# Index queries of a sparse-attention layer: from rows of tokens to columns of tokens, and only for tokens 64 to 255

## The chip, the core and the metric

The kernel runs on one core of one Trainium2 chip. The metric is the device time of one execution in microseconds (us); a comparison of two kernels is a ratio of such times, taken on the same chip. The engines of the core have short names throughout: PE is the matrix engine (PEld its weight loads), V or DVE the vector engine, A or ACT the scalar engine, G or POOL the GpSimd engine, SP the engine whose queue issues the loads from memory.

## What is computed

The reference is two layers of a decoder trunk on 256 tokens of width 1024. A layer is a half-step feed-forward block, a mixer, and another half-step feed-forward block. The mixer projects the normed tokens once and feeds three groups of attention heads. The change concerns the group A, whose 4 query heads attend only to keys that an indexer picks:

```python
iq = apply_rope(iq.reshape(B, S, IDX_HEADS, IDX_DIM), cos, sin)     # 8 indexer heads of 64
ik = apply_rope(ik.reshape(B, S, 1, IDX_DIM), cos, sin)[:, :, 0]    # one shared indexer key
...
topk = min(DSA_TOPK_MAX, S // 4)                                    # 64
idx_logits = jnp.einsum('bqhe,bse->bqhs', qib, ki_f)
score = jnp.einsum('bqh,bqhs->bqs', wib * DSA_IDX_SCALE, jax.nn.relu(idx_logits))
score = jnp.where(causal[None], score, -jnp.inf)
_, sel = lax.top_k(score, topk)
valid = sel <= qpos[None, :, None]
```

A query at position p has p + 1 admissible keys. For the first 64 positions that is at most 64, so the 64 picked keys contain all of them and what is attended to is the causal mask itself, whatever the scores are.

## The kernel before

Tokens stand on partitions, in two tiles of 128 (t = 0, 1). Each weight is split into a high and a low part (`wh` by an ACT cast, L125; `wl` by a DVE subtraction, L129), and so are the normed activations (`norm.h`, `norm.l`, two halves of one tile `norm.x`); a product is three matmuls, high by high, high by low and low by high (`mm3`, L340, over `mm`, L338). The splitting is kept ahead of use by a small planner (`Weights`, L64): `take()` hands out the next unit, `pump()` (L101) puts one more cast on ACT and one subtraction, a unit behind, on DVE, unless seven units are already ahead. A unit has 1024 columns in most places, 672 in the chunk `ib` and 768 in the chunk `a`.

The mixer (L688) goes through eight chunks of the input projection in the order of `CHUNKS` (L51): iq, ib, b, a, ck, cq, cv, cg. A chunk has four units of weights and each unit is one step: 12 matmuls, in which 128 tokens are the stationary operand and up to 512 features the moving one, so that a result has tokens on partitions. Beside the chunks runs other work of the mixer: `at_step(n, fn)` (L692) puts a function on a list, and `run_side()` (L695) after each unit issues those whose step has come. This is program order; each engine then works through its own instructions strictly in that order, and an instruction that waits holds up all that is behind it on its engine.

What happens to the index queries (`post_iq`, L760) after the four steps of the chunk iq: ACT copies the two banks to four tiles of 128x256 with the norm's factor (`evac`, L737); `rope` (L704) turns them by position along the free dimension, with two products on G into a tile `swapped` (L710, L711; two such tiles in turn, shared with all other uses of `rope`) and a product and a sum on DVE (L712, L713); at step 9 PE transposes them in 16 pieces of 64 rows (L179), and ACT copies the result to `iqT`, features on partitions and tokens along the free dimension.

After the chunk ib, at step 8, `post_ib` (L773) issues the same for the single index key: `rope` on `ix` (L786, through L710 to L713), then a copy that doubles it into `ikd` (L787). At step 10 PE transposes `ikd` (`turn_ik`, L818, the transposes in L821), at step 11 it computes the products of `iqT` and `ikT` for the second tile of queries (`index(1)`, L826), and DVE sums them into `score` (L842). At step 18 (`B_TURN`) the same is done for the first tile, and in steps 15 to 30 `topk` takes the largest eight scores eight times over. `amask` (L858) makes the mask of the A heads from what was taken.

At the start of the mixer the second half of the normed activations is still to be made: `norm.half(1)` (L376), with eight PE transposes (L373), runs within the first step, and `norm.sums()` after the second.

Of the kernel before, what the change touches and what calls it, by code (L numbers as in the profile page):

```python
# [10 lines left out]
F32 = mybir.dt.float32  # L11
# [3 lines left out]
ALU = mybir.AluOpType  # L15
# [3 lines left out]
P = 128  # L19
S = 256  # L20
# [4 lines left out]
DEPTH = 2  # L25
HD = 64
TOPK = 64
EPS = 1e-6
NEG = -1e30
IDX_SCALE = (8 ** -0.5) * (64 ** -0.5)  # L30
# [20 lines left out]
CHUNKS = [  # L51
    ("iq", [(384, 512, 0)]),
    ("ib", [(896, 328, 0), (3272, 8, 328)]),
    ("b", [(1224, 512, 0)]),
    ("a", [(0, 384, 0)]),
    ("ck", [(2248, 512, 0)]),
    ("cq", [(1736, 512, 0)]),
    ("cv", [(2760, 512, 0)]),
    ("cg", [(3280, 512, 0)]),
# [94 lines left out]
def kernel(ctx: ExitStack, tc: tile.TileContext, x, ffn1_norm, ffn1_w_gate, ffn1_w_up, ffn1_w_down,  # L154
# [3 lines left out]
    cp = ctx.enter_context(tc.tile_pool(name="cp", bufs=1))  # L158
# [3 lines left out]
    hp = ctx.enter_context(tc.tile_pool(name="hp", bufs=HID_BUFS))  # L162
    tp = ctx.enter_context(tc.tile_pool(name="tp", bufs=9))
    sm = ctx.enter_context(tc.tile_pool(name="sm", bufs=4))
    at = ctx.enter_context(tc.tile_pool(name="at", bufs=1))
# [5 lines left out]
    V, A, G, T = nc.vector, nc.scalar, nc.gpsimd, nc.tensor  # L171

    def bank(tag):
        return psum.tile([P, 512], F32, name="ps_" + tag, tag=tag)

    def turn(ps, i, src):
        for e, b in enumerate(ps):
            r = slice(64 * e, 64 * e + 64)
            T.transpose(b[:, 64 * i:64 * i + 64], src[r], ident[r, r])  # L179

    def turned(ps, dst, copies):
        for e, copy in enumerate(copies):
            d = dst[..., 64 * e:64 * e + 64]
            n = 64
            for k in d.shape[1:-1]:
                n *= k
            src = ps[e][:, :n]
            if len(d.shape) == 3:
                src = src.rearrange("p (b j) -> p b j", j=64)
            else:  # L190
                src = src.rearrange("p (a b j) -> p a b j", a=d.shape[1], j=64)
            copy(d, src)

    def by_block(ap):
        return ap.rearrange("p h (t c) -> p (h t) c", c=P)
# [3 lines left out]


    trunk = xp.tile([P, 2, D], F32, name="trunk")
    cst = cp.tile([P, 384], F32, name="cst")
    ident = cp.tile([P, P], F32, name="ident")
    rows, more_rows = tmp(P)[:16], tmp(P)[:32]
    gT = cp.tile([P, 48], F32, name="gT")
# [32 lines left out]
    W = Weights(tc, raw_pool, split_pool)  # L238
# [85 lines left out]

    future = cst[:, 0:P]
    cs = cst[:, P:3 * P].rearrange("p (t c) -> p t c", t=2)
    causal = cp.tile([P, 3 * P], F32, name="causal")
    cqa = [at.tile([P, 8, HD], F32, name=f"cqa{t}", tag=f"cqa{t}") for t in range(2)]
    cka = [at.tile([P, 8, HD], F32, name=f"cka{t}", tag=f"cka{t}") for t in range(2)]
# [15 lines left out]
    def rsqrt(dst, src, per, n, tag):  # L345

        y = sm.tile([P, 32], F32, name="y_" + tag, tag="y_" + tag, bufs=1)[:, :n]
        V.tensor_scalar(dst, src, per, EPS, op0=ALU.mult, op1=ALU.add)  # L348
        G.tensor_tensor(y, dst, minus_half[:, :n], op=ALU.pow)  # L349
# [338 lines left out]
    def mixer(l, norm, nxt):  # L688
        side, count = [], itertools.count()
        step = [0]  # L690

        def at_step(n, fn):  # L692
            side.append((n, next(count), fn))
# [7 lines left out]
        def heads(ap, n):  # L701
            return ap.rearrange("p (h d) -> p h d", h=n)

        def rope(x, ta, tb, E=G):  # L704

            n = x.shape[1]
            bc = lambda a: a[:, None, :].to_broadcast([P, n, a.shape[1]])
            b = tp.tile([P, S], F32, name="swapped", tag="swapped", bufs=2)
            b = heads(b[:, :n * HD], n)
            G.tensor_tensor(b[:, :, 0:32], x[:, :, 32:64], bc(tb[:, 0:32]), op=ALU.mult)  # L710
            G.tensor_tensor(b[:, :, 32:64], x[:, :, 0:32], bc(tb[:, 32:64]), op=ALU.mult)  # L711
            E.tensor_tensor(x, x, bc(ta), op=ALU.mult)  # L712
            E.tensor_tensor(x, x, b, op=ALU.add)  # L713
# [22 lines left out]
        def evac(dst, ps, t, scale=None):  # L736
            A.activation(dst, ps, AF.Copy, scale=norm.r[:, t:t + 1])  # L737
# [3 lines left out]
        def pairs_T(dst, *xs):  # L741

            ps = [bank("acc") for _ in range(2)]
            i = itertools.count()
            for x in xs:
                for j in range(0, x[0].shape[1], P):
                    for t in range(2):
                        turn(ps, next(i), x[t][:, j:j + P])
            turned(ps, by_block(dst), (A.copy, A.copy))
# [7 lines left out]
        st = {}  # L757


        def post_iq(ps):  # L760
            rot = [[hp.tile([P, S], F32, name="iqr", tag="hl") for _ in range(2)] for t in range(2)]
            for t in range(2):
                for jj in range(2):
                    evac(rot[t][jj], ps[t][:, jj * S:(jj + 1) * S], t)
                    rope(heads(rot[t][jj], 4), cs[:, t, 0:64], cs[:, t, 64:128], V)

            def turn_iq():
                st["iqT"] = at.tile([P, 4, S], F32, name="iqT", tag="kT")
                pairs_T(st["iqT"], *[[rot[t][jj] for t in range(2)] for jj in range(2)])

            at_step(9, turn_iq)

        def post_ib(ps):  # L773
            ss = sm.tile([P, 2, 4], F32, name="ssbq", tag="ss")
# [3 lines left out]
            small = [at.tile([P, 80], F32, name=f"ix{t}", tag=f"ix{t}") for t in range(2)]  # L778
            rot = [hp.tile([P, S], F32, name="bqr", tag="hl") for _ in range(2)]
# [4 lines left out]
            for t in range(2):  # L784
                x = small[t][:, None, 0:64]
                rope(x, cs[:, t, 0:64], cs[:, t, 64:128], V)  # L786
                V.tensor_copy(ikd[t], x.to_broadcast([P, 2, HD]))  # L787
                V.tensor_tensor(fg[:, t], small[t][:, 72:80], fb[:, l], op=ALU.add)
                V.tensor_scalar(st["iw"][:, t], small[t][:, 64:72], IDX_SCALE, None, op0=ALU.mult)
            sq = []  # L790
            for t in range(2):
                evac(rot[t], ps[t][:, 72:328], t)
# [65 lines left out]
            def amask():  # L858
                am = at.tile([P, 3 * P], F32, name="amask", tag="amask")
                V.tensor_scalar(am[:, P:2 * P], st["score"][1][:, 0:P], -2e38, None, op0=ALU.is_gt)  # L860
                for t in range(2):
                    V.scalar_tensor_tensor(am[:, 2 * t * P:(2 * t + 1) * P], st["score"][t][:, t * P:(t + 1) * P],
                                           -2e38, future, op0=ALU.is_gt, op1=ALU.max)
                V.tensor_scalar(am, am, NEG, None, op0=ALU.mult)
                st["amask"] = am

            for r in range(TOPK // 8):
                at_step(TOP_STEP + 2 * r, lambda: topk(1))
# [288 lines left out]
        def both_scores(_):  # L1157
            for fn in (scores, st["B"][0]):
                for p in range(2):
# [4 lines left out]
                    b=lambda p: st["B"][1](p), B=lambda p: st["B"][2](p), T=lambda _: tanh(), w=causal_part)  # L1164
# [6 lines left out]
        at_step(A_STEP + 1, lambda: do("q j"))  # L1171

        oT = {}
        posts = dict(iq=post_iq, ib=post_ib, a=post_a, b=post_b, ck=post_ck, cq=post_cq, cv=post_cv, cg=post_cg)
        for name, cols in CHUNKS:
            n = sum(c[1] for c in cols)
            ps = [bank("gu") for _ in range(2)]
            for u in range(4):
                w = W.take()
                for kk in range(2):  # L1180
                    k = 2 * u + kk
                    for t in range(2):
                        ts = slice(t * P, (t + 1) * P)
                        mm3(ps[t][:, :n], (norm.h[:, k, ts], norm.l[:, k, ts]), [v[:, kk] for v in w],
                            k == 0, k == KT - 1)
                    if name == "iq" and k == 0:
                        norm.half(1)
                if name == "iq" and u == 1:
                    norm.sums()
                step[0] += 1  # L1190
                run_side()
                if step[0] < A_STEP:
                    W.pump(2 if name == "iq" else 1)
            posts[name](ps)
        while side:
            step[0] += 1
# [63 lines left out]
        def norm_out(_):  # L1260
# [5 lines left out]
            for t in range(2):  # L1266
# [3 lines left out]
                    p=lambda _: W.pump(), Z=residuals, N=norm_T, M=norm_out)  # L1270
# [21 lines left out]
    norm = Norm(0, 0)  # L1292
    turn_gains()
    for l in range(DEPTH):
        norm = ffn(norm, lambda: Norm(1, l), lambda: before_mixer(l), l == 0)
        norm = mixer(l, norm, lambda: Norm(2, l))
        norm = ffn(norm, (lambda: Norm(0, l + 1)) if l + 1 < DEPTH else None)
# [7 lines left out]
def _constants(np):  # L1305

    inv = (1.0 / np.power(10000.0, np.arange(0, HD, 2, dtype=np.float64) / HD)).astype(np.float32)
    ang = np.arange(S, dtype=np.float32)[:, None] * inv[None, :]
    c, s = np.cos(ang), np.sin(ang)
    rot = np.concatenate([c, c, -s, s], axis=1).astype(np.float32).reshape(2, P, P)  # L1310
    i = np.arange(P)
    return np.ascontiguousarray(np.concatenate([i[None, :] > i[:, None], rot[0], rot[1]], axis=1), dtype=np.float32)


# [17 lines left out]
```

## Time and profile before

| | |
|---|---|
| median of three runs | 1008.81 us (1008.67 to 1008.81) |
| span of the profiled execution | 1007.0 us |
| first index-query matmul to the transpose of `ikd`, layer 1 | 192.04 to 217.51 us of the span |
| the same, layer 2 | 690.35 to 715.82 us |

The profile belongs to one execution. It gives no time of its own beside the span; the span runs from its first to its last instruction, and the runs' times are 1.7 to 1.8 us longer than that. The chain of waits is followed back from the last instruction, each time to what released it. A row of the timeline has the start and the length in us, the engine, the line, the operation, what it writes and reads, the shape and how many instructions of the same kind it merges; the last entry, in brackets, is the idle time before it and what ended it. Lengths of matmuls are modelled ends, so what a matmul costs in a stream is read from the distance of starts.

### The profile page before, as it was taken

What the parts mean: (1) busy time and instruction counts of PE and PEld (TensorE: products, weight loads), DVE (VectorE), ACT (ScalarE), POOL (GpSimd) and SP (SyncE); (2) the same over time, 40 slices, a digit from 0 to 9 for tenths busy, and PEclk for the clock granted to TensorE, in tenths of its full rate; (3) what the DMA queues carried; (4) which work ended last, traced back from release to release, by engine and by line L of the source; (5) the groups of instructions that cost most, each with busy time, mean ns of one, the idle gap of its engine ahead of it and who ended that gap; (6) DMA issues with size and microseconds to landing.
All of it is one profiled execution on the core that took longest, in us unless ns stands there. A gap on an engine that the chain in (4) does not pass through costs nothing.

```text
span 1007.0 us, 15203 instructions
## 1 busy us (share of the span) xinstructions
PE 1002.5 (100%) x5692; PEld 857.6 (85%) x5692; DVE 795.0 (79%) x1474; ACT 590.6 (59%) x1090; POOL 164.5 (16%) x192
## 2 busy tenths in 40 slices
PE   9999999999999999999999999999999999999998
PEld 8888888888878888888888888888887788888887
DVE  5978778779998777777878777787899877777775
ACT  6655555567776555555465555556678765555552
POOL 2003000068812000000000020001778120000000
PEclk9999999999999999999999999999999999999999
DMA  9764746464625455655645655665556255374731
GB/s 289 264 225 157 233 147 237 140 241 168 221 94 168 156 178 174 203 188 199 199 168 180 203 182 195 197 197 175 182 204 230 72 179 170 131 242 141 237 127 42
DMA packets 133497, 184.60 MB, mean 183 GB/s; under 512 B 7152, under 2 KB 106928, under 8 KB 133424
## 3 DMA queue, kind: packets, MB, share of 16 engines
q1 hardware_dynamic: 133392, 183.62, 55.1%
q8 instruction: 45, 0.74, 0.3%
q14 instruction: 28, 0.23, 0.1%
q10 hardware_dynamic: 32, 0.01, 0.0%
HBM read 182.55 MB, written 1.06 MB: 182 GB/s over the span
## 4 chain that ended last, share of the span: by engine, by line
PE 98%; DVE 1%; ACT 0%; issue 0%; POOL 0%; POOLq 0%
PE ps_gu L338 67%; PE ps_acc L338 29%; PE ps_acc L373 1%; PE ps_acc L179 1%; DVE wl L129 0%; PE ps_gu L179 0%; DVE p L1078 0%; PE ps_acc L535 0%; DVE ol L1138 0%; PE ps_acc L940 0%; PE ps_acc L400 0%; DVE cT L1240 0%; DVE cT L1236 0%; ACT oh L1130 0%; PE ps_acc L821 0%; PE ps_acc L875 0%
## 5 line engine op out<-in xcount | busy, mean ns | idle before, releaser
L129 DVE TENSOR_TENSOR wl<-raw,wh 128x1024 fp32r<-128x1024 f32 (+2 forms) x342 | 416.9, 1229 | 25.2 <-ACT wh L125 25.1
L125 ACT CAST wh<-raw 128x1024 fp32r<-128x1024 f32 (+2 forms) x341 | 341.7, 1036 | 19.1 <-PE ps_gu L338 9.3
L338 PE MATMUL ps_gu<-xhl,wh 128*128 128x512 f32 x1408 | 330.8, 390 | 0.0
L338 PEld LDWEIGHTS ps_gu<-xhl,wh 128*128 128x128 f32 x1408 | 263.1, 188 | 54.0 <-ACT wh L125 0.4
L338 PEld LDWEIGHTS ps_gu<-xhl,wl 128*128 128x128 f32 x1408 | 176.0, 191 | 4.0
L338 PE MATMUL ps_gu<-xhl,wl 128*128 128x256 f32 x1408 | 178.7, 283 | 0.0
L482 DVE TENSOR_TENSOR tmp<-ps_gu,tmp 128x256 f32<-128x256 f32 x176 | 72.9, 423 | 108.9 <-ACT tmp L481 108.6
L338 PE MATMUL ps_gu<-wh,xhl 128*128 128x512 f32 (+2 forms) x512 | 155.1, 378 | 0.0
L338 PE MATMUL ps_acc<-wh,hh 128*128 128x512 f32 (+1 forms) x352 | 137.2, 390 | 0.0
L338 PE MATMUL ps_acc<-wl,hh 128*128 128x512 f32 (+1 forms) x352 | 137.1, 389 | 0.0
L338 PE MATMUL ps_acc<-wh,hl 128*128 128x512 f32 (+1 forms) x352 | 136.5, 388 | 0.0
L481 ACT COPY tmp<-ps_gu 128x256 f32<-128x256 f32 x176 | 63.4, 371 | 91.5 <-PE ps_gu L338 91.2
L338 PEld LDWEIGHTS ps_gu<-wh,xhl 128*128 128x128 f32 x512 | 94.6, 188 | 16.8 <-issue 1.7
L496 ACT CAST hh<-tmp 128x256 fp32r<-128x256 f32 x80 | 32.6, 407 | 120.3 <-DVE tmp L493 120.3
L338 PE MATMUL ps_gu<-wl,xhl 128*128 128x512 f32 (+2 forms) x256 | 95.7, 374 | 0.0
L488 ACT ACTIVATE tmp<-tmp 128x256 f32<-128x256 f32 x88 | 36.9, 419 | 83.3 <-DVE tmp L486 83.1
L349 POOL TENSOR_TENSOR y_n<-msq,minus_half 128x2 f32<-128x2 f32 x6 | 7.0, 1174 | 443.8 <-DVE msq L348 443.8
L338 PEld LDWEIGHTS ps_acc<-wh,hl 128*128 128x128 f32 x352 | 66.1, 188 | 13.9
L338 PEld LDWEIGHTS ps_acc<-wh,hh 128*128 128x128 f32 x352 | 66.2, 188 | 12.6
L338 PEld LDWEIGHTS ps_acc<-wl,hh 128*128 128x128 f32 x352 | 66.3, 188 | 12.4 <-DVE wl L129 0.2
L338 PEld LDWEIGHTS ps_gu<-wl,xhl 128*128 128x128 f32 x256 | 48.2, 188 | 6.9
L506 DVE TENSOR_TENSOR tmp<-tmp,rb 128x256 f32<-128x256 f32 x88 | 37.5, 426 | 3.0
(232 smaller groups left out, 899.2 us busy)
## 6 DMA issues: line engine op xcount, KB each, us to landing
raw<-in_ffn_w_down_dram SPq DMA_DIRECT2D x44, 1024.0 KB, 4.9
raw<-in_ffn_w_gate_dram SPq DMA_DIRECT2D x42, 1024.0 KB, 6.9
raw<-in_ffn_w_up_dram SPq DMA_DIRECT2D x42, 1024.0 KB, 7.7
raw<-in_w_in_dram SPq DMA_DIRECT2D x24, 1024.0 KB, 5.0
raw<-in_w_out_dram SPq DMA_DIRECT2D x8, 1024.0 KB, 5.0
raw<-in_w_in_dram SPq DMA_DIRECT2D x4, 768.0 KB, 4.9
raw<-in_w_in_dram SPq DMA_DIRECT2D x4, 656.0 KB, 4.0
raw<-in_ffn_w_gate_dram SPq DMA_DIRECT2D x3, 512.0 KB, 7.7
```

Source lines behind the costliest of these rows:

```text
L125: self.nc.scalar.copy(hv, src)
L129: (engine or self.nc.vector).tensor_tensor(lv, self.srcs[self.n_low], hv.bitcast(F32), op=ALU.subtract)
L179: T.transpose(b[:, 64 * i:64 * i + 64], src[r], ident[r, r])
L338: T.matmul(o, l, r, start=start, stop=stop, skip_group_check=True)
L349: G.tensor_tensor(y, dst, minus_half[:, :n], op=ALU.pow)
L373: T.transpose(ps[:, i, t * P:(t + 1) * P], trunk[:, t, (2 * mp + i) * P:(2 * mp + i + 1) * P], ident)
L481: A.copy(o, ps[:, 1])
L482: V.tensor_tensor(o, ps[:, 0], o, op=ALU.add)
L488: A.activation(th, t_, AF.Tanh, scale=0.5)
L496: (V.tensor_copy if late else A.copy)(hh, t_)
L506: V.tensor_tensor(t_, t_, norm.rb, op=ALU.mult)
```

## The change

The chunk iq leaves the loop over chunks. A new function does it in four steps ahead of the loop, with the weights as the stationary operand (128 features at a time, f = 0 to 3) and the tokens 64 to 255 as the moving one: one matmul of 2 x 192 columns takes high and low activations against the high weights, one of 192 columns takes the high activations against the low weights. The result has features on partitions and needs no transposition. The rotation then acts along partitions: G multiplies 32 partitions at a time, with the other half's partitions as input, in 16 instructions of 32x192 for the four f; DVE does four products and four sums of 128x192. The columns of `iqT` of the first 64 tokens are set to zero. The norm's factor is left out of the queries and put on the indexer's head weights instead. In the mask the first 64 rows are copied from the causal one. The constants get two more tables of 192 columns.

```diff
-        def post_iq(ps):
-            rot = [[hp.tile([P, S], F32, name="iqr", tag="hl") for _ in range(2)] for t in range(2)]
-            for t in range(2):
-                for jj in range(2):
-                    evac(rot[t][jj], ps[t][:, jj * S:(jj + 1) * S], t)
-                    rope(heads(rot[t][jj], 4), cs[:, t, 0:64], cs[:, t, 64:128], V)
-
-            def turn_iq():
-                st["iqT"] = at.tile([P, 4, S], F32, name="iqT", tag="kT")
-                pairs_T(st["iqT"], *[[rot[t][jj] for t in range(2)] for jj in range(2)])
-
-            at_step(9, turn_iq)
+        def index_queries():
+
+            ps = [bank("gu")[:, :2 * LATE].rearrange("p (a s) -> p a s", a=2) for _ in range(4)]
+            qs = [hp.tile([P, S], F32, name="iqr", tag="hl")[:, :LATE] for _ in range(4)]
+            iqT = st["iqT"] = at.tile([P, 4, S], F32, name="iqT", tag="kT")
+            G.memset(iqT[:, :, :TOPK], 0.0)
+            for u in range(4):
+                w = W.take()
+                for f in range(4):
+                    fs = slice(f * P, (f + 1) * P)
+                    for kk in range(2):
+                        mm(ps[f], w[0][:, kk, fs], norm.x[:, 2 * u + kk, :, TOPK:], u + kk == 0, False)
+                    for kk in range(2):
+                        mm(ps[f][:, 0], w[1][:, kk, fs], norm.h[:, 2 * u + kk, TOPK:], False, u + kk == 4)
+                    if u == 0 and f == 1:
+                        norm.half(1)
+                    if u == 3:
+                        o = tmp(LATE)
+                        A.copy(o, ps[f][:, 1])
+                        V.tensor_tensor(qs[f], ps[f][:, 0], o, op=ALU.add)
+                if u == 1:
+                    norm.sums()
+                step[0] += 1
+                run_side()
+                W.pump(2)
+            swapped = [tp.tile([P, S], F32, name="swapped", tag="swapped", bufs=2)[:, :LATE] for _ in range(2)]
+
+            def turned_part(f):
+                b = swapped[f % 2]
+                for i in range(4):
+                    to, of = slice(32 * i, 32 * i + 32), slice(32 * (i ^ 1), 32 * (i ^ 1) + 32)
+                    G.tensor_tensor(b[to], qs[f][of], csT[of, 1], op=ALU.mult)
+
+            def straight_part(f):
+                V.tensor_tensor(iqT[:, f, TOPK:], qs[f], csT[:, 0], op=ALU.mult)
+
+            def added(f):
+                V.tensor_tensor(iqT[:, f, TOPK:], iqT[:, f, TOPK:], swapped[f % 2], op=ALU.add)
+
+            for f in range(2):
+                turned_part(f)
+            for f in range(4):
+                straight_part(f)
+            for f in range(2):
+                at_step(5, lambda f=f: added(f))
+                at_step(5, lambda f=f: turned_part(2 + f))
+                at_step(7, lambda f=f: added(2 + f))
...
-                V.tensor_scalar(st["iw"][:, t], small[t][:, 64:72], IDX_SCALE, None, op0=ALU.mult)
+                V.tensor_scalar(st["iw"][:, t], small[t][:, 64:72], IDX_SCALE, norm.r[:, t:t + 1], op0=ALU.mult,
+                                op1=ALU.mult)
...
+                V.tensor_copy(am[:TOPK, 0:P], future[:TOPK])
                 for t in range(2):
-                    V.scalar_tensor_tensor(am[:, 2 * t * P:(2 * t + 1) * P], st["score"][t][:, t * P:(t + 1) * P],
-                                           -2e38, future, op0=ALU.is_gt, op1=ALU.max)
+                    r = slice(TOPK if t == 0 else 0, P)
+                    V.scalar_tensor_tensor(am[r, 2 * t * P:(2 * t + 1) * P], st["score"][t][r, t * P:(t + 1) * P],
+                                           -2e38, future[r], op0=ALU.is_gt, op1=ALU.max)
...
-        for name, cols in CHUNKS:
+        index_queries()
+        for name, cols in CHUNKS[1:]:
...
-                    W.pump(2 if name == "iq" else 1)
+                    W.pump()
```

`TOPK` is 64 and `LATE` is 192. The products of `iqT` and `ikT`, the sums of the scores and the rounds of `topk` keep their number and sizes.

More of the change, by code (lines that the diff above doesn't have):

```diff
@@ L27 @@
 TOPK = 64
+LATE = S - TOPK
 EPS = 1e-6
@@ L201 @@
     trunk = xp.tile([P, 2, D], F32, name="trunk")
-    cst = cp.tile([P, 384], F32, name="cst")
+    cst = cp.tile([P, 3 * P + 2 * LATE], F32, name="cst")
     ident = cp.tile([P, P], F32, name="ident")
@@ L326 @@
     cs = cst[:, P:3 * P].rearrange("p (t c) -> p t c", t=2)
+    csT = cst[:, 3 * P:].rearrange("p (i s) -> p i s", i=2)
     causal = cp.tile([P, 3 * P], F32, name="causal")
@@ L1173, in mixer @@
         oT = {}
-        posts = dict(iq=post_iq, ib=post_ib, a=post_a, b=post_b, ck=post_ck, cq=post_cq, cv=post_cv, cg=post_cg)
-        for name, cols in CHUNKS:
+        posts = dict(ib=post_ib, a=post_a, b=post_b, ck=post_ck, cq=post_cq, cv=post_cv, cg=post_cg)
+        index_queries()
+        for name, cols in CHUNKS[1:]:
             n = sum(c[1] for c in cols)
@@ L1185, in mixer @@
                             k == 0, k == KT - 1)
[L1186 to L1189, printed above, removed]
                 step[0] += 1
@@ L1311, in _constants @@
     i = np.arange(P)
-    return np.ascontiguousarray(np.concatenate([i[None, :] > i[:, None], rot[0], rot[1]], axis=1), dtype=np.float32)
+    late = np.concatenate([np.concatenate([c, c, c, c], axis=1).T, np.concatenate([s, -s, s, -s], axis=1).T], axis=0)
+    late = late.reshape(2, P, S)[:, :, TOPK:].transpose(1, 0, 2).reshape(P, 2 * LATE)
+    return np.ascontiguousarray(np.concatenate([i[None, :] > i[:, None], rot[0], rot[1], late], axis=1),
+                                dtype=np.float32)
 def kernel(**inputs):
```

## The prediction

> **What bounds the kernel now.** I read the page first: its busy times and the chain of waits.
>
> ```profile
> span 1007.0 us, 15203 instructions
> PE 1002.5 (100%) x5692; PEld 857.6 (85%) x5692; DVE 795.0 (79%) x1474; ACT 590.6 (59%) x1090; POOL 164.5 (16%) x192
> PE 98%; DVE 1%; ACT 0%; issue 0%; POOL 0%; POOLq 0%
> ```
>
> The chain is PE from end to end, so matmul time removed is gained at once, unless PE afterwards arrives somewhere before its input does. POOL's 16% is an average; the next view, sums by stretch, shows the stretch in question, from the first index-query matmul (192.04) to the end of the chunk ib.
>
> ```profile
> core 0: us, PE busy (x) PEld busy (x) DVE busy (x) ACT busy (x) POOL busy (x), PEclk, DMA share, GB/s
> 192.04:203.81 11.77, 11.77 (x57) 9.84 (x56) 10.20 (x15) 9.51 (x18) 1.21 (x1) 1.00 0.41 130
> 203.81:211.20 7.39, 7.39 (x50) 7.38 (x49) 5.85 (x11) 4.82 (x10) 4.02 (x8) 1.00 0.80 291
> ```
>
> The clock is full (1.00), the index queries take PE 11.77 us, ib 7.39. DVE is busy for 10.20 of the first 11.77. What PE meets next is read from the timeline, of PE and of DVE, in both layers:
>
> ```profile
> 192.04 0.39 PE L338 MATMUL ps_gu<-wh,xhl 128*128 128x512 f32 x1
> 217.51 0.38 PE L821 MATMUL ps_acc<-ident,ikd 128*128 128x128 f32 x2
> 690.35 0.39 PE L338 MATMUL ps_gu<-wh,xhl 128*128 128x512 f32 x1
> 715.82 0.38 PE L821 MATMUL ps_acc<-ident,ikd 128*128 128x128 f32 x2
> 209.48 4.21 DVE L129 TENSOR_TENSOR wl<-raw,wh 128x1024 fp32r<-128x1024 f32 x4
> 213.61 0.27 DVE L712 TENSOR_TENSOR ix<-ix,cst 128x64 f32<-128x64 f32 x1
> 215.39 0.78 DVE L787 COPY ikd<-ix 128x128 f32<-128x128 f32 x1
> ```
>
> This is what decides. The transpose of `ikd` starts at 217.51, and DVE has `ikd` ready at 215.39 + 0.78 = 216.17: PE arrives only 1.34 us after its input. DVE took the index key up at 213.61, behind four splits of weights. Counted from the first index-query matmul (I call that time T), PE is at T+25.47 and `ikd` at T+24.13, and in layer 2 PE is at T+25.47 again. What the change saves on PE beyond 1.34 us is worth nothing if `ikd` stays where it is, and costs if `ikd` moves back.
>
> **PE's part.** Distances of starts price a matmul in a stream.
>
> ```profile
> 153.67 3.83 PE ps_gu L338 x32
> 177.71 10.88 PE ps_acc L338 x48
> 228.19 0.33 PE L338 MATMUL ps_gu<-wl,xhl 128*128 128x384 f32 x1
> 232.87 0.33 PE L338 MATMUL ps_gu<-wl,xhl 128*128 128x384 f32 x1
> 274.08 0.60 PE L940 MATMUL ps_acc<-ident,aqr 128*128 128x128 f32 x4
> 274.51 0.38 PE L940 MATMUL ps_acc<-ident,akd 128*128 128x128 f32 x2
> ```
>
> The first two are pieces of the chain: 32 matmuls of 256 columns (the feed-forward block's narrow ones) at 0.120 us each, 48 of 512 at 0.227. Between the next two lie nine groups of three of 384 columns: 4.68 / 27 = 0.173. A line through these gives 0.093 at 192 columns. But four 128-column transposes start 0.109 apart (0.43 / 4), longer than their columns alone would take by that line: a load of new weights with each instruction seems to set a floor. I take 0.109. Before, 48 matmuls x 0.227 = 10.88. After, 32 x 0.173 + 32 x 0.109 = 9.03. With the 0.86 us of the eight transposes of `norm.half(1)`, which both kernels have in this stage, the queries end at T+9.89 instead of T+11.77. `half(1)` stands after 8 of the new matmuls (1.13 us) where it stood after 6 of the old (1.36), so what follows it on ACT and DVE is 0.23 earlier too, and its results are still due only at the third unit, over 3 us later: free.
>
> ```profile
> 213.69 0.39 PE L338 MATMUL ps_gu<-wh,xhl 128*128 128x512 f32 x1
> 214.01 0.71 PE L179 MATMUL ps_acc<-ident,iqr 64*128 64x64 f32 x16
> 214.65 0.50 PE L338 MATMUL ps_gu<-wh,xhl 128*128 128x512 f32 x1
> 214.99 0.39 PE L338 MATMUL ps_gu<-wl,xhl 128*128 128x512 f32 x1
> ```
>
> The transposes of the queries go: from 213.69 to 214.99 is 1.30, of which two matmuls are 0.45, so 0.85 us.
>
> Something comes back at once. The new function takes all four banks of its kind, so ib must wait until DVE has summed the first.
>
> ```profile
> 198.66 4.66 DVE L129 TENSOR_TENSOR wl<-raw,wh 128x672 fp32r<-128x672 f32 x5
> 192.85 1.22 DVE L129 TENSOR_TENSOR wl<-raw,wh 128x1024 fp32r<-128x1024 f32 x1
> 206.06 0.41 DVE L712 TENSOR_TENSOR iqr<-iqr,cst 128x256 f32<-128x256 f32 x1
> ```
>
> Four of the five splits of the first row are queued ahead of these sums (the fourth step's is behind). They end at 203.32 less some 1.2 for the last, T+10.06, with the shift T+9.83. By the other two rows DVE needs (1.22 - 0.41) / 768 = 1.055 ns a column and 0.14 us besides, so 0.34 for a sum of 192. ib starts at T+10.17 instead of T+9.89. Then 7.39 for ib and 24 x 0.227 = 5.44 for two steps of b: PE stands before `ikd` at **T+23.0**, against T+25.47. That is the whole gain, 2.47 us a layer.
>
> **When `ikd` is ready.** DVE must do, in order: the sums, a split, four straight products, two `added`, two splits, two `added`, two splits, and then the index key. Each `added` waits for four instructions of G, and G for DVE (the third and fourth `turned_part` write buffers that `added` has read). So all 16 instructions of G lie ahead of `ikd`, where there were 8 shorter ones.
>
> ```profile
> 203.95 0.46 POOL L710 TENSOR_TENSOR swapped<-iqr,cst 128x128 f32<-128x128 f32 x1 [3.85 <-ACT iqr L737]
> 204.37 0.46 POOL L711 TENSOR_TENSOR swapped<-iqr,cst 128x128 f32<-128x128 f32 x1
> 220.05 0.73 POOL L713 TENSOR_TENSOR bqr<-bqr,swapped 128x256 f32<-128x256 f32 x1
> 217.31 1.25 POOL L711 TENSOR_TENSOR swapped<-bqr,tab 128x128 f32<-128x128 f32 x1
> 217.29 2.09 DVE L129 TENSOR_TENSOR wl<-raw,wh 128x768 fp32r<-128x768 f32 x2
> 211.91 0.97 POOL L711 TENSOR_TENSOR swapped<-ix,cst 128x32 f32<-128x32 f32 x1
> ```
>
> Alone, G needs 0.46 us for 128 columns and 0.73 for 256: 2.1 ns a column and 0.19 besides. While DVE runs splits (two inputs from SBUF), the 128 columns take 1.25, and 32 columns 0.97. So the two engines take turns, and their columns add up. A check on before: from G's first (203.95) to DVE's taking up `ix` (213.61), 9.66 us, DVE did 8 x 256 + 2 x 1024 + 2 x 768 = 5632 columns (5.94 us) and G 8 x 128 + 3 x 32 = 1120 (2.35), together 8.29; the other 1.37 are fixed parts and waits. From there to `ikd` were 2.56.
>
> After, from G's first at about T+10.3: DVE 1024 + 4 x 192 + 4 x 192 + 2 x 1024 + 2 x 768 = 6144 columns, 6.48 us; G 16 x 192 + 96 = 3168 columns, 6.65; together 13.1. That assumes that 32 partitions cost G what 128 do; no row shows fewer than 128. With nothing for fixed parts `ix` is taken up at T+23.4 and `ikd` is ready at T+26.0; stretched as before (9.66 / 8.29) it is T+25.6 and T+28.2. Laid out instruction by instruction, one engine after the other on its columns and 0.07 (DVE) or 0.15 (G) ahead of each, the kernel before gives T+24.2 (measured 24.13) and the changed one **T+27.5**. I take that, being nearest to a measured case. PE, there at T+23.0, waits 4.5 us and goes on 2.1 us later than before.
>
> Nothing behind that is due sooner than PE: the profile has DVE idle before the scores, so its delay is taken up there.
>
> ```profile
> 222.37 0.48 DVE L842 SCALAR_TENSOR_TENSOR score<-tmp,iw,causal 128x256 f32<-128x256 f32 x1 [2.99 <-ACT tmp L838]
> ```
>
> The rest I cost at nothing: ACT's four 128x192 copies for four of 128x256, and two of 128x512 dropped (ACT is at 59%); the memset on an idle G; the head weights' second factor; the small copy in `amask`; the larger constants, one load in the feed-forward block before. With cover gone the copy in `amask` would be 0.3 us a layer.
>
> **Sum.** 2 x (+2.1) = +4.2 us on the profiled span of 1007.0, and as both lie 1.8 apart, on the median 1008.8: **1013.0 us**. Its own range goes from no fixed parts (2 x 0.5: 1009.8) to 1016 (stretched as before, 2 x 2.7, and some more for G).
>
> **Rivals.**
>
> First, *faster*: the four quarter instructions of a `turned_part` touch different partitions and overlap, or cost less than whole ones. If the 16 take under 0.3 us each instead of 0.56 (192 x 2.1 ns + 0.15), `ikd` is ready by T+23 and all 2.47 us land in each layer: 1008.8 - 4.9 = 1003.9. Against it: in the rows of G independent instructions start 0.42 apart where one lasts 0.46, hardly any overlap; but those use all partitions. The Trainium skill, "GPSIMD Engine Reference", section Instruction dispatch, says that a core of G serves 16 fixed partitions and starts the next instruction as soon as its own share is done. By that the quarters would overlap, and the result would be this rival's; no row here shows it. I give 0.25.
>
> Second, *much slower*: all matmuls of the trace on split operands (written as fp32r, as the rows of L129 show) have 256 columns or more; the only shorter matmuls that are not transposes are plain fp32, at another price.
>
> ```profile
> 220.57 2.00 PE L338 MATMUL ps_acc<-ikT,iqT 64*128 64x256 f32 x16
> 222.50 0.50 PE L338 MATMUL ps_gu<-wh,xhl 128*128 128x512 f32 x1
> ```
>
> Eight products of 256 columns, two at a time, take 1.93 us: 0.48 a pair. If 192 columns in fp32r went at that pace, 0.36 instead of 0.109, the queries would end at T+17.9 and PE reach `ikd` at T+30.7; laid out the same way it is ready at T+33.8, +8.4 us a layer, 1025.6; with G's overlap +5.3, 1019.4. For it is only that no row speaks against it; the 256-column row, the nearest, lies on the line. I give 0.20.
>
> Third, *no difference*: G somewhat cheaper, 1.5 ns a column, so that the wait (2 us) eats the gain: 1008. I give 0.10.
>
> That leaves 0.45 for the forecast.
>
> **How the numbers follow.** A measurement here tells 0.2%, 2 us, from no change. Faster: the first rival, 0.25. Same: the third and the forecast's lower edge, 0.13. Slower: the rest, 0.62. The range runs from the first rival's 1003.9, a little lower for a narrow matmul on the line, to the second's milder case: 1003.3 to 1019.5; what is left out is the second rival's worse case, 0.15, and some of the tails.
>
> **What would show it.** In the changed profile: starts of the 192-column matmuls about 0.11 apart; ib's first matmul near T+10.2; G's 32x192 at 0.6 us, longer beside splits, the last ending near T+22.4; and PE idle for some 4.5 us before L821 in each layer, with DVE and POOL in the chain there. If PE does not wait there and stands at T+23, the price of G was wrong; if the queries end at T+18, the price of the narrow matmul.

## The result and the profile after

The changed kernel takes 1020.83 us (median of four runs, 1019.68 to 1021.4), the kernel before 1008.74: 1.0119 times as long, 95% interval 1.0104 to 1.0133. The forecast was 1013.0 with a range up to 1019.5. The sign was right; the size was some three times what was forecast.

The changed kernel's lines are numbered anew: `mm` is L340, the splits L130, G's quarter products L793, DVE's straight products L796, `added` L799, the copy into `ikd` L824, its transposes L859, the scores L880.

The profile page of the changed kernel, its span, busy times and chain:

```profile
span 1019.7 us, 15219 instructions
PE 1003.7 (98%) x5692; PEld 860.0 (84%) x5692; DVE 801.0 (79%) x1484; ACT 586.7 (58%) x1086; POOL 180.8 (18%) x210
PE 91%; DVE 3%; POOL 3%; issue 1%; DMA 1%; ACT 1%; SPq 0%; POOLq 0%; DVEq 0%
```

PE's share of the chain has gone from 98% to 91%; DVE's has gone from 1% to 3% and POOL's from 0% to 3%. The timeline of PE shows where: the query matmuls, the start of ib, the transposes of `ikd` in layer 1, and the first score products.

```profile
197.41 0.54 PE L340 MATMUL ps_gu<-xhl,wh 128*128 128x384 f32 x2
...
197.98 0.54 PE L340 MATMUL ps_gu<-xhl,wh 128*128 128x384 f32 x2
...
202.22 0.42 PE L340 MATMUL ps_gu<-wh,xhl 128*128 128x336 f32 x1
...
214.93 0.39 PE L340 MATMUL ps_gu<-wh,xhl 128*128 128x512 f32 x1
219.12 0.47 PE L859 MATMUL ps_acc<-ident,ikd 128*128 128x128 f32 x1 [3.80 <-DVE ikd L824]
220.86 0.47 PE L859 MATMUL ps_acc<-ident,ikd 128*128 128x128 f32 x1 [1.27 <-DVE ikd L824]
...
221.56 0.63 PE L340 MATMUL ps_gu<-wl,xhl 128*128 128x512 f32 x1
221.99 1.05 PE L340 MATMUL ps_gu<-wh,xhl 128*128 128x512 f32 x2
222.84 0.63 PE L340 MATMUL ps_gu<-wl,xhl 128*128 128x512 f32 x1
...
226.17 1.13 PE L340 MATMUL ps_acc<-ikT,iqT 64*128 64x256 f32 x8
```

One f of the queries costs 197.98 - 197.41 = 0.57 (forecast 2 x 0.173 + 2 x 0.109 = 0.564). T is 191.99 here, so ib starts at T+10.23 (forecast T+10.17), and after its last matmul before `ikd`, at 214.93 + 0.23 = 215.16, PE stands at T+23.2 (forecast T+23.0). PE's part is as the prediction had it. Then PE waits 3.80 and 1.27 us for `ikd`. Layer 2 shows the same pair of waits.

```profile
723.99 0.33 PE L859 MATMUL ps_acc<-ident,ikd 128*128 128x128 f32 x1 [3.80 <-DVE ikd L824]
725.74 0.47 PE L859 MATMUL ps_acc<-ident,ikd 128*128 128x128 f32 x1 [1.42 <-DVE ikd L824]
```

What the prediction had no term for stands behind the waits: three matmuls of 512 columns from 221.56 to 222.84 take 1.28 us, 0.427 each, where the same instruction took 0.227. The sums by stretch name the reason, first of the changed kernel, then of the kernel before:

```profile
215.00:220.00 5.00, 0.79 (x3) 0.18 (x1) 3.76 (x10) 0.00 (x0) 4.47 (x8) 0.90 0.42 134
220.00:225.00 5.00, 4.14 (x11) 3.27 (x12) 4.62 (x9) 1.32 (x2) 4.76 (x6) 0.50 0.54 197
225.00:230.00 5.00, 5.00 (x28) 3.70 (x27) 1.86 (x4) 2.67 (x5) 2.13 (x3) 0.91 0.63 210
```

```profile
220.00:225.00 5.00, 5.00 (x30) 3.70 (x29) 2.35 (x5) 3.26 (x6) 2.81 (x3) 1.00 0.62 210
```

The column ahead of the last two is the granted clock. It is 0.50 from 220 to 225; narrow stretches of this trace read either 1.00 or 0.50, so a missing share counts twice, and PE spends about 2 x 0.10 x 5 + 5 + 2 x 0.09 x 5 = 6.9 us at half clock, a part of it in the waits themselves.

Why `ikd` is late is read from G and DVE (timelines of the changed kernel, then the view of line L793 over both layers, with the least, the median and the longest duration in ns):

```profile
202.31 13.80 POOL L793 TENSOR_TENSOR swapped<-iqr,cst 32x192 f32<-32x192 f32 x16 [2.50 <-DVE iqr L781]
```

```profile
204.00 2.77 DVE L796 TENSOR_TENSOR iqT<-iqr,cst 128x192 f32<-128x192 f32 x4
...
208.69 0.36 DVE L799 TENSOR_TENSOR iqT<-iqT,swapped 128x192 f32<-128x192 f32 x1 [1.17 <-POOL swapped L793]
...
213.29 0.36 DVE L799 TENSOR_TENSOR iqT<-iqT,swapped 128x192 f32<-128x192 f32 x1 [1.16 <-POOL swapped L793]
216.14 0.36 DVE L799 TENSOR_TENSOR iqT<-iqT,swapped 128x192 f32<-128x192 f32 x1 [2.49 <-POOL swapped L793]
...
220.04 0.77 DVE L824 COPY ikd<-ix 128x128 f32<-128x128 f32 x1
```

```profile
L793 POOL TENSOR_TENSOR swapped<-iqr,cst x32: 582/600/1591, 202.3 to 720.4; 32x192 f32<-32x192 f32 x32
```

G's sixteen instructions end at 216.11, T+24.1 (13.80 us from the first start to the last end; the row merges them, and they are busy for 12.7 of it); DVE has waited 1.17 + 1.16 + 2.49 = 4.82 us for them, and its own straight products, with two inputs from SBUF, take 2.77 / 4 = 0.69 each where the fourth `added`, alone, takes 0.36. The index key stands behind all this, and the second half of `ikd` is ready at 220.81, T+28.8.

What each step is worth comes out of the place of the same instruction in the two traces, in each layer counted from its own T (before 192.04 and 690.35, after 191.99 and 696.87). Layer 2 stands in brackets:

| instruction | later by |
|---|---|
| second transpose of `ikd` (before 217.62, after 220.86) | 3.29 (3.28) |
| first score product (220.57, 226.17): the clock adds | 2.36 (2.49) |
| everything after it in the mixer adds | 0.93 (0.37) |
| sum | 6.58 (6.14) |

The two layers give 12.72, less the 0.05 by which T comes earlier in layer 1: 12.67, the difference of the spans (1019.68 - 1007.01). Of the last step, 0.36 and 0.41 arise at the second transposes of c_T, and 0.60 in layer 1 in the output projection, where PE waits for G's `ohl`.

### The profile page after: what moved, and what is told of

It reads as the page before. It is cut to its first block, busy times and chain, and to the rows that moved or that the text cites. A ratio compares the mean times of both kernels' runs of the same rounds, so it can differ in the third digit from the quotient of the medians.

```text
span 1019.7 us, 15219 instructions
## 1 busy us (share of the span) xinstructions
PE 1003.7 (98%) x5692; PEld 860.0 (84%) x5692; DVE 801.0 (79%) x1484; ACT 586.7 (58%) x1086; POOL 180.8 (18%) x210
## 4 chain that ended last, share of the span: by engine, by line
PE 91%; DVE 3%; POOL 3%; issue 1%; DMA 1%; ACT 1%; SPq 0%; POOLq 0%; DVEq 0%
PE ps_gu L340 60%; PE ps_acc L340 29%; POOL swapped L793 3%; DVE wl L130 2%; DMA raw<-in_ffn_w_up_dram 1%; PE ps_acc L375 1%; PE ps_acc L180 1%; ACT p L1100 0%; PE ps_gu L180 0%; DVE p L1118 0%; DVE xhl L367 0%; SPq L100 0%; POOL tmp L1142 0%; SPq L225 0%; ACT xhl L364 0%
## 5 line engine op out<-in xcount | busy, mean ns | idle before, releaser
L130 DVE TENSOR_TENSOR wl<-raw,wh 128x1024 fp32r<-128x1024 f32 (+2 forms) x342 | 419.1, 1234 | 25.3 <-ACT wh L126 25.2
L340 PE MATMUL ps_gu<-xhl,wh 128*128 128x512 f32 (+1 forms) x1472 | 347.7, 389 | 0.7 <-ACT wh L126 0.4
L340 PEld LDWEIGHTS ps_gu<-xhl,wh 128*128 128x128 f32 x1472 | 272.7, 188 | 54.8 <-ACT wh L126 0.8
L340 PEld LDWEIGHTS ps_gu<-xhl,wl 128*128 128x128 f32 x1472 | 187.5, 192 | 4.1 <-DVE wl L521 0.2
L340 PE MATMUL ps_gu<-xhl,wl 128*128 128x256 f32 (+1 forms) x1472 | 190.3, 283 | 0.0
L340 PE MATMUL ps_gu<-wh,xhl 128*128 128x512 f32 (+2 forms) x448 | 138.0, 384 | 0.1
L340 PE MATMUL ps_acc<-wh,hh 128*128 128x512 f32 (+1 forms) x352 | 137.4, 390 | 0.0
L340 PE MATMUL ps_acc<-wl,hh 128*128 128x512 f32 (+1 forms) x352 | 137.2, 390 | 0.0
L340 PE MATMUL ps_acc<-wh,hl 128*128 128x512 f32 (+1 forms) x352 | 136.7, 388 | 0.0
L340 PEld LDWEIGHTS ps_gu<-wh,xhl 128*128 128x128 f32 x448 | 85.0, 193 | 15.3 <-issue 1.7
L340 PE MATMUL ps_gu<-wl,xhl 128*128 128x512 f32 (+2 forms) x224 | 85.1, 380 | 0.0
L340 PEld LDWEIGHTS ps_acc<-wh,hl 128*128 128x128 f32 x352 | 66.2, 188 | 13.8
L340 PEld LDWEIGHTS ps_acc<-wh,hh 128*128 128x128 f32 x352 | 66.3, 188 | 12.6
L340 PEld LDWEIGHTS ps_acc<-wl,hh 128*128 128x128 f32 x352 | 66.3, 188 | 12.3 <-DVE wl L130 0.2
L340 PEld LDWEIGHTS ps_gu<-wl,xhl 128*128 128x128 f32 x224 | 43.3, 193 | 6.0
```

The costliest lines, as they stand in the source:

```text
L130: (engine or self.nc.vector).tensor_tensor(lv, self.srcs[self.n_low], hv.bitcast(F32), op=ALU.subtract)
L340: T.matmul(o, l, r, start=start, stop=stop, skip_group_check=True)
```

## The experiments

Theory W: G's quarter instructions and DVE hold each other up, so `ikd` comes late and PE, which now comes early, waits; the wait makes the clock fall, and that is the missing cost. Rivals were that the new matmuls cost more, that the loss lies behind the index queries, and that it is spread over other edits.

**e1_filled: the wait filled with matmuls that nobody reads.** All else as in the changed kernel.

```diff
-                ps = bank("acc")[:, :S]
+                full = bank("acc")
+                for i in range(22):
+                    mm(full, norm.h[:, 0, 0:P], norm.x[:, 0], True, True)
+                ps = full[:, :S]
```

> The changed kernel, with 22 more matmuls of 512 columns ahead of the transposes of the index key, into the bank that these overwrite (5.0 us of PE work in the place where PE waits 5.1 us). Theory W (G's 16 instructions and DVE shut each other out, the index key comes late, PE waits, and on top of it the granted clock halves after the wait, so that 12 matmuls of 512 columns start 0.427 us apart instead of 0.227): the wait is filled, the key comes no later, the clock stays at 1, and 2.3 us a layer are gained: about 1016 us against 1020.8. If the clock's fall has another cause, or costs nothing: 1021. If the added matmuls simply add up: 1031.

1016.62 us (1016.47 to 1016.86), ratio 1.0079 (1.0064 to 1.0094), 4.2 less than the changed kernel. PE in its timeline:

```profile
214.84 5.15 PE L340 MATMUL ps_acc<-xhl 128*128 128x512 f32 x22
...
220.63 0.33 PE L862 MATMUL ps_acc<-ident,ikd 128*128 128x128 f32 x1 [0.52 <-DVE ikd L824]
...
221.03 0.40 PE L340 MATMUL ps_gu<-wl,xhl 128*128 128x512 f32 x1
221.26 0.63 PE L340 MATMUL ps_gu<-wh,xhl 128*128 128x512 f32 x2
```

`ikd` is no earlier, but the matmuls behind start 0.23 apart: work that is thrown away makes the kernel faster, because the clock stays up. The clock's share is 4.2 us by the median times and 4.9 by the spans of the two profiled executions, against 2.36 + 2.49 = 4.85 in the table.

**e2_no_turn and e3_whole: without G's quarter instructions, and with whole ones.** The first leaves out the crosswise half of the rotation, G's 16 instructions and DVE's 4 sums; the second multiplies all 128 partitions at once, so the halves are not exchanged.

```diff
-            for f in range(2):
-                turned_part(f)
...
-            for f in range(2):
-                at_step(5, lambda f=f: added(f))
-                at_step(5, lambda f=f: turned_part(2 + f))
-                at_step(7, lambda f=f: added(2 + f))
```

> The changed kernel without the 16 instructions of G and the four sums that take them up; the index queries are left with the straight part of the rotation alone. Theory W: the index key is ready before PE asks for it (some T+21), the whole PE gain of 2.47 us a layer lands, 1003.5 to 1004.5 us. Rival R (the feature-major matmuls, their 64 loads and four banks, lose the time): at least 1015. Rival Q (DVE's own queue of splits and products delays the key, G does not matter): about 1017.

```diff
-                for i in range(4):
-                    to, of = slice(32 * i, 32 * i + 32), slice(32 * (i ^ 1), 32 * (i ^ 1) + 32)
-                    G.tensor_tensor(b[to], qs[f][of], csT[of, 1], op=ALU.mult)
+                G.tensor_tensor(b, qs[f], csT[:, 1], op=ALU.mult)
```

> The changed kernel with one G instruction of 128x192 in place of four of 32x192 in each turned part, reading the same partitions that it writes (so the halves aren't exchanged, a different product). Theory W, with a quarter instruction costing what a whole one costs: G has 4 instead of 16, 864 columns instead of 3168, the key is ready near T+22.5, and the gain lands: 1003.5 to 1006. If quarters cost a quarter, this changes nothing: 1021.

1004.61 us, ratio 0.9959 (0.9945 to 0.9974), and 1004.70, ratio 0.9960 (0.9945 to 0.9975). In e2_no_turn the transposes of `ikd` start without a wait:

```profile
215.14 0.38 PE L853 MATMUL ps_acc<-ident,ikd 128*128 128x128 f32 x2
```

That is 2.37 us before the 217.51 of the kernel before. So up to `ikd` the matmuls, `half(1)`, the head weights and the larger constants do what the prediction says, and the narrow matmul as rival is out; at the second transposes of c_T some 0.35 us a layer is lost again here too. The whole 16 us between this run and the changed kernel hang on the crosswise half, and not on DVE's four sums, which e3_whole still has. G's rows in e3_whole:

```profile
202.20 1.17 POOL L791 TENSOR_TENSOR swapped<-iqr,cst 128x192 f32<-128x192 f32 x2 [2.43 <-DVE iqr L781]
205.94 3.48 POOL L791 TENSOR_TENSOR swapped<-iqr,cst 128x192 f32<-128x192 f32 x2 [2.57 <-DVE iqT L797]
```

A whole instruction of 128x192 takes about 0.6 (two in 1.17), as much as a quarter of 32x192 (median 0.600): four quarters cost four wholes. The second pair, beside two splits of DVE, takes 3.48, three times as long as the first.

**e8_half: half of G's instructions.** The crosswise half is left out for two of the four f.

```diff
-                at_step(5, lambda f=f: turned_part(2 + f))
-                at_step(7, lambda f=f: added(2 + f))
```

> The changed kernel with the crosswise half of the rotation left out for two of the four groups of features: 8 instructions of G of 32x192 instead of 16, 2 sums of DVE instead of 4, all else the same. Theory W (the price is a wait for ikd plus a clock that falls only after a long wait): ikd is ready some 5 us earlier, at about T+23.5 to T+24, PE waits at most 1 us, the clock stays full, and the time is 1004.7 to 1006.5, so that the second eight instructions cost 14 to 16 us of time though they last about 10 and lie off the chain. Rival: each instruction of G costs the same share; then the time is halfway between the kernel without the turn (1004.6) and the changed one (1020.8), 1012.7.

1005.23 us, ratio 0.9967 (0.9955 to 0.9980), as theory W had it; halfway by count would be 1012.7. PE waits 0.31 for `ikd`:

```profile
215.34 0.33 PE L857 MATMUL ps_acc<-ident,ikd 128*128 128x128 f32 x1 [0.31 <-DVE ikd L822]
```

The first eight instructions, with their two sums, cost 0.6 us of time, the second eight 15.6. It is a threshold, not a price per instruction: the time is lost only where `ikd` comes later than PE.

**e4_act_swap: the exchange given to ACT.** ACT copies the 32-partition pieces into the exchanged places, G multiplies in place with four whole instructions, DVE subtracts; nothing is left out.

```diff
-                    G.tensor_tensor(b[to], qs[f][of], csT[of, 1], op=ALU.mult)
+                    A.copy(b[to], qs[f][of])
+                G.tensor_tensor(b, b, csT[:, 1], op=ALU.mult)
...
-                V.tensor_tensor(iqT[:, f, TOPK:], iqT[:, f, TOPK:], swapped[f % 2], op=ALU.add)
+                V.tensor_tensor(iqT[:, f, TOPK:], iqT[:, f, TOPK:], swapped[f % 2], op=ALU.subtract)
```

> The same result as the changed kernel, but ACT exchanges the halves (16 copies of 32x192 to other partitions), and G multiplies whole tiles of 128x192 in place, 4 instructions; the sums become differences. Theory W: 16 copies of some 0.3 us on ACT, which shares no port with DVE, 4 x 0.6 on G; key near T+23, PE there at T+23: 1004 to 1006, faster than the kernel before. If ACT, now with 5 us more a layer ahead of its casts, delays the weights: PE waits there, 1008 or more.

1007.85 us, ratio 0.9994 (0.9984 to 1.0003): no difference from before, 13 us less than the changed kernel. ACT, and behind it DVE and PE:

```profile
203.16 5.94 ACT L793 COPY swapped<-iqr 32x192 f32<-32x192 f32 x16
209.12 2.52 ACT L126 CAST wh<-raw 128x1024 fp32r<-128x1024 f32 x3
```

```profile
210.20 1.23 DVE L130 TENSOR_TENSOR wl<-raw,wh 128x1024 fp32r<-128x1024 f32 x1 [1.90 <-ACT wh L126]
```

```profile
216.50 0.33 PE L860 MATMUL ps_acc<-ident,ikd 128*128 128x128 f32 x1 [1.41 <-DVE ikd L825]
...
216.90 0.39 PE L340 MATMUL ps_gu<-wl,xhl 128*128 128x512 f32 x1
217.13 0.62 PE L340 MATMUL ps_gu<-wh,xhl 128*128 128x512 f32 x2
```

The sixteen copies, 5.94 us in a row, now hold up a cast, the cast a split, and the split the index key by 1.90. A wait of 1.41 before `ikd` is left; after it the matmuls start 0.23 apart, so this wait cost no clock.

**e5_late: the transposes of `ikd` two steps later.** Only where PE meets `ikd` is moved.

```diff
-            at_step(10, turn_ik)
+            at_step(12, turn_ik)
...
-            at_step(11, lambda: index(1))
+            at_step(13, lambda: index(1))
```

> The changed kernel with the transposes of ikd two steps later (step 12 instead of 10) and the score products of the second tile at step 13 instead of 11; nothing is left out. In the changed kernel PE stood still 3.8 and 1.3 us before these transposes, and the twelve matmuls behind them started 0.427 apart instead of 0.227. Theory W (the loss is that PE comes too early, and the halved clock follows from standing still): with 24 more matmuls, 5.4 us, ahead of them, PE comes at T+28.6 when ikd is ready at T+28.8; the wait is under 0.4, the matmuls behind start 0.23 apart, the saving on PE (2.1 to 2.5 us a layer) stays less 0.35 a layer lost later: 1004 to 1006. Rival L (what is lost is owed to DVE, which is late with everything behind the index queries): the scores and the rounds of topk then come later still, PE waits at the A heads instead, and the time stays at 1008 or above.

1012.78 us, ratio 1.0042 (1.0028 to 1.0056). Theory W's number, 1004 to 1006, failed, and rival L's stands: the wait at `ikd` has gone (the transposes start at 220.52, right behind a matmul), but PE meets new ones further on: 0.47 us for G's `bkr` at 238.5, and 30 us after `ikd` a long one before the transposes of `lf`, whose bank DVE still reads.

```profile
220.52 0.63 PE L859 MATMUL ps_acc<-ident,ikd 128*128 128x128 f32 x2
...
251.67 0.38 PE L915 MATMUL ps_acc<-ident,lf 128*8 128x128 f32 x2 [2.17 <-DVE nm L1090]
...
252.36 1.04 PE L340 MATMUL ps_gu<-wh,xhl 128*128 128x512 f32 x2
...
253.62 1.05 PE L340 MATMUL ps_gu<-wh,xhl 128*128 128x512 f32 x2
```

After these 2.17 us of waiting the clock falls too (252.36 to 253.62 is 1.26 for three matmuls; the row at 253.62 is the next pair). In layer 2 of the same run PE waits 2.14 us at this place and the clock does not fall; the last section comes back to that. The instructions of DVE that free that bank, in e5_late and in the kernel before:

```profile
251.13 0.48 DVE L1090 CUSTOM_DVE_ANT_0 tmp<-ps_acc,causal,minus_b 128x256 f32<-128x256 f32 x1
```

```profile
249.99 0.48 DVE L1050 CUSTOM_DVE_ANT_0 tmp<-ps_acc,causal,minus_b 128x256 f32<-128x256 f32 x1
```

and the first of the transposes in the kernel before:

```profile
250.95 0.27 PE L875 MATMUL ps_acc<-ident,lf 128*8 128x128 f32 x1
```

DVE is 1.14 us later than before, and PE, which started these transposes at 250.95, now stands before them from 249.50 on. In the kernel before DVE stood idle for 2.99 and 1.79 us before the scores; in e5_late the timeline marks no idle time of it between `ikd` and this place.

**e9_one_later and e10_half_late: one step later, and two steps later with half of G's work.** The first is e5_late with steps 11 and 12; the second is e8_half with the edit of e5_late, so half of the crosswise products are left out.

> The changed kernel with the transposes of ikd at step 11 and the score products of the second tile at step 12, one step later than in the changed kernel and one earlier than in e5_late; nothing is left out. e5_late showed a wait of 2.17 us after which matmuls start 0.427 apart, e4_act_swap one of 1.41 after which they do not. Theory W: 12 matmuls, 2.7 us, more stand ahead, so PE waits 1.1 and then 1.2 us in two pieces, each too short for the clock to fall; at the score products PE is within 0.5 of its place in the kernel before, DVE is as late as in e5_late but PE comes later to the transposes of lf than it did there, so the wait there is under 1 us, and the time is 1007.5 to 1010.5. Rival: the clock falls all the same, and the time is 1012 or more, as in e5_late.

> The kernel e8_half (half of the crosswise rotation left out, 8 instructions of G instead of 16) with the transposes of ikd at step 12 and the score products of the second tile at step 13, as in e5_late. Rival S (the loss in e5_late comes of having put the scores and with them the rounds of topk two steps later): the wait before the transposes of lf is here too, 1008 or more. Theory L (the loss in e5_late is the time that DVE stood behind G, which the two steps did not take away): DVE is some 4 us earlier here, there is no wait there, and the time is 1003.5 to 1005.5.

e9_one_later: 1013.48 us, ratio 1.0048 (1.0033 to 1.0063). The two waits are as expected, but the clock falls (221.59 to 222.87 is again 1.28 for three matmuls):

```profile
219.13 0.33 PE L859 MATMUL ps_acc<-ident,ikd 128*128 128x128 f32 x1 [1.10 <-DVE ikd L824]
220.87 0.33 PE L859 MATMUL ps_acc<-ident,ikd 128*128 128x128 f32 x1 [1.41 <-DVE ikd L824]
...
221.59 1.06 PE L340 MATMUL ps_gu<-wh,xhl 128*128 128x512 f32 x2
...
222.87 1.05 PE L340 MATMUL ps_gu<-wh,xhl 128*128 128x512 f32 x2
```

So theory W was wrong in taking each wait by itself; 1.10 and 1.41 with one transpose between count together.

e10_half_late: 1006.18 us, ratio 0.9977 (0.9967 to 0.9986), between the two numbers given. In its trace DVE stands idle again for 2.62 us before the scores and PE waits 0.33 before `lf`:

```profile
249.31 0.38 PE L913 MATMUL ps_acc<-ident,lf 128*8 128x128 f32 x2 [0.33 <-DVE nm L1088]
```

So the loss of e5_late is for the greater part DVE's time lost to G (6.6 us of time between the two kernels); a smaller part does come of putting the scores later, since e10_half_late is 0.95 slower than e8_half.

**e6_act_later and e7_act_later_mask: the exchange on ACT and one step later; and the mask as before.** e6_act_later is e4_act_swap with steps 11 and 12. e7_act_later_mask takes back the change in `amask` besides:

```diff
-                V.tensor_copy(am[:TOPK, 0:P], future[:TOPK])
...
-                    r = slice(TOPK if t == 0 else 0, P)
-                    V.scalar_tensor_tensor(am[r, 2 * t * P:(2 * t + 1) * P], st["score"][t][r, t * P:(t + 1) * P],
-                                           -2e38, future[r], op0=ALU.is_gt, op1=ALU.max)
+                    V.scalar_tensor_tensor(am[:, 2 * t * P:(2 * t + 1) * P], st["score"][t][:, t * P:(t + 1) * P],
+                                           -2e38, future, op0=ALU.is_gt, op1=ALU.max)
```

> The kernel e4_act_swap (ACT copies the exchanged 32-partition pieces, four whole instructions of G multiply in place) with the transposes of ikd at step 11 instead of 10 and the score products of the second tile at step 12 instead of 11; nothing is left out. In e4_act_swap PE waited 1.4 us a layer before the second transpose. Theory W: one step (2.7 us) more ahead of it covers that wait, so all of the saving on PE arrives there: 1007.9 less 2 x 1.4 to 2 x 1.75, 1004.3 to 1005.0, the time of the kernel without the turn. Rival L: the wait only moves to a later place where DVE is due, and the time stays at 1007.9.

> The kernel e6_act_later with the mask made as in the kernel before: two instructions of 128 rows and no copy of the causal rows. The zero scores of the first 64 tokens still enter topk. If the small copy in the mask is what costs 0.35 us a layer at the second transposes of c_T, this is 0.7 faster than e6_act_later. If that loss comes from elsewhere on DVE (the work around the queries), the time is that of e6_act_later within 0.2.

1004.38 us (1004.04 to 1004.51), ratio 0.9958 (0.9945 to 0.9970), and 1003.93 (1003.76 to 1004.13), ratio 0.9954 (0.9940 to 0.9967). The transposes of `ikd` in e6_act_later start without a wait:

```profile
217.59 0.39 PE L340 MATMUL ps_gu<-wh,xhl 128*128 128x512 f32 x1
217.82 0.38 PE L860 MATMUL ps_acc<-ident,ikd 128*128 128x128 f32 x2
```

That is the time of the kernel without the crosswise half, with nothing left out: 4.2 us below the kernel before and 16 below the changed one. The mask brings another 0.45, less than the 0.7 expected, and little beside the spread (the two ranges touch): at the second transposes of c_T e6_act_later loses 0.11 us in layer 1 and 0.56 in layer 2, e7_act_later_mask nothing and 0.26. So the copy is a part of that loss, and what the rest is stays open.

## Why the prediction was right in sign and wrong in size

- **The narrow and wide matmuls, `half(1)`, the transposes removed, ib waiting for DVE**: right. ib starts at T+10.23 for T+10.17, and e2_no_turn shows 2.32 us gained at `ikd`, counted from T, for 2.47. The second rival (0.36 per narrow matmul) is refuted: four matmuls of one f take 0.57 together.
- **The first rival (quarters overlap or are cheap)**: refuted. Sixteen take 13.80 us, and where DVE runs no split one starts some 0.67 us after the other, no less than one lasts; e3_whole shows a quarter at the price of a whole. What the Trainium skill, "GPSIMD Engine Reference", section Instruction dispatch, says of cores that serve fixed partitions does not show up as overlap here.
- **Price of G, "32 partitions cost G what 128 do"**: right, 0.600 against 0.56. **Turns with DVE**: right in kind. G's sixteen end at T+24.1 instead of T+22.4, since the layout allowed 12.1 us for what took 13.8; DVE is then 0.4 quicker than laid out. `ikd` is ready at T+28.8 instead of T+27.5. In the table this is 3.29 and 3.28 a layer for 2.1: 2.4 us in all.
- **"Goes on 2.1 us later than before"** is the step that failed. It prices a wait at its length, as if PE went on at full pace. There was no term for the clock, which falls to 0.50 with such a wait and costs 2.36 and 2.49 us more a layer; e1_filled takes that away and gains 4.2. The upper end of the forecast's own range, 1016, had no room for it either. That the result lies close above the whole range's end, 1019.5, is chance: that end was the price of slow narrow matmuls, which did not come about.
- **"Nothing behind that is due sooner than PE"**: true in the changed kernel only because PE itself was late; there PE meets no wait at `lf`. Where PE isn't late (e5_late) DVE's lost time comes due at `lf`. The copy in `amask` was put at nothing, or 0.3 a layer with cover gone; by e7_act_later_mask, where the exchange is on ACT, it is worth some 0.2 a layer. The later places add 0.93 and 0.37 in all; why G's `ohl` is late in layer 1, and what else acts at c_T, stays open.
- **The sum**: 4.2 forecast + 2.4 (`ikd` later) + 4.85 (clock) + 1.3 (later places) - 0.05 = 12.7 on the spans.
- **The third rival (no difference)** came about in e4_act_swap, but in another way: G cheaper, ACT's casts later.

## What to carry to other kernels

Before PE time is taken away, look at how much earlier the next input from another engine is than PE: here 1.34 us, and the same change lost 12 us with its consumer in the old place and won 4.2 with the exchange on another engine and the consumer one step later. Price a wait of PE at its length and, from some 2 us on, count with a stretch at half clock besides (2.4 us a layer here), and add up waits that lie close together; between 1.4 and 2.2 us no rule by length alone holds here. Work cut by partitions on G costs as many full instructions as there are pieces (0.600 us for 32x192, about 0.6 for 128x192).

## What the runs showed of the hardware

How long the clock stays down is read from the sums by stretch, of e9_one_later and of e5_late:

```profile
220.00:225.00 5.00, 4.13 (x12) 3.28 (x13) 4.93 (x10) 1.32 (x2) 4.75 (x6) 0.66 0.55 199
```

```profile
251.60:255.00 3.40, 3.33 (x11) 2.64 (x12) 3.33 (x12) 1.59 (x5) 0.77 (x1) 0.61 0.43 122
255.00:260.00 5.00, 5.00 (x22) 4.06 (x21) 4.90 (x18) 1.93 (x7) 4.92 (x4) 0.92 0.39 161
```

By the missing share, counted twice: 2 x 0.34 x 5 = 3.4 us in the first, 2 x 0.39 x 3.4 + 2 x 0.08 x 5 = 3.45 in the second, 6.9 in the changed kernel. So the clock comes down for 3.4 us or twice that. The Trainium skill, "TensorE: Matmul & The Clock Gate", Part 1, says that a free-running window of 3413 ns decides and that PE knows half and full clock only; the lengths agree with it. It puts the fall after an idle window of about 3.4 us. Here less did: 2.17 us of waiting in layer 1 of e5_late, and 1.10 and 1.41 close together, 2.51 in all, in e9_one_later, while 1.41 alone did not. But the length alone does not decide. In layer 2 of e5_late PE waits 2.14 us and the clock stays at 1.00:

```profile
752.45 0.38 PE L915 MATMUL ps_acc<-ident,lf 128*8 128x128 f32 x2 [2.14 <-DVE nm L1090]
```

```profile
752.40:755.80 3.40, 3.35 (x16) 2.80 (x17) 3.33 (x10) 1.58 (x5) 0.79 (x1) 1.00 0.45 120
```

An estimate from these traces and that window of 3413 ns makes sense of it. Narrow stretches place the falls at 219.03 and 724.20 in the changed kernel, 505.17 us or 148 windows apart, and at 252.37 in e5_late. Counted on from there, a border of windows falls at 750.71, into the wait of layer 2 (750.31 to 752.45), and 1.73 us of it lie in one window; the wait of layer 1 (249.50 to 251.67) lies whole in the window that ends with the fall. In layer 2 of e9_one_later the clock falls at 723.15, and the window that ends there holds 1.78 us of its two waits. So PE standing still for about half of a window would bring the clock down, and a wait of some 2 us would cost more or less by where it happens to lie. No run was made to test this. In the changed kernel the second wait, 1.27 us, lies in the first window at half clock, which a second one follows; in e5_late and e9_one_later PE does not wait there, and the clock comes back after one.

G beside DVE: the same instruction of 32x192 took 0.582 to 1.591 us, and two of 128x192 took 1.17 or 3.48. The Trainium skill, "SBUF — State Buffer", section Who interferes with whom, says that a DVE instruction with two SBUF inputs contends with one of G that reads SBUF, and calls contention for the ports that they share an exclusive lock. The lengthening on both sides (on DVE the straight products take 0.69, where an `added` of the same size alone takes 0.36) agrees with that.
